# An encoder block whose instructions keep the program's order from the second gate on, with output blocks taken in pairs

## The chip, the cores and the metric

One core of one Trainium2 chip runs the whole kernel in one launch. The metric is the device time of that launch in microseconds. The kernel before took 1429.65 us, the median of three runs (1428.54 to 1430.14).

## The reference

One encoder block for 256 tokens of width 2048, in float32, cut to its products:

```python
h = rms_norm(x, g_mix); proj = h @ w_in              # q, k, v of three mixers, and 3 gates x 2048
oa = dilated windows (6 heads); ob = grouped attention (6 heads, 2 of k and v)
mkv = rms_norm(mem, g_mem) @ w_mem_kv                # 2048 -> 512 keys + 512 values
oc = cross-attention to mem (4 heads)
merged = gate0 * (oa @ w_br_a) + gate1 * (ob @ w_br_b) + gate2 * (oc @ w_br_c)   # gates: sigmoid
x = x + merged @ w_o                                 # 2048 x 2048
hf = rms_norm(x, g_ffn) @ w_ffn_in                   # 2048 -> 2 x 5632
x = x + (silu(hf[..., :5632]) * hf[..., 5632:]) @ w_ffn_out
```

## The kernel before

**Precision.** Every float32 operand goes as two float32r parts: `whi`, a rounded copy made by ACT (`split`, L86), and `wlo`, the remainder by DVE (L87). A product is three matmuls: high by high, high by low, low by high. So each weight costs ACT one pass and DVE one, and PE three for each half of the tokens (128 of 256). `xT`, `memT`, `mT`, `x1T`, `hT` are the stationary operands, transposed and split the same way; `rawT` is an operand as it is loaded.

**A plain product** (`product`, L161) makes 512 output columns: it loads four 128-row blocks of weights at a time (`raw`, 1 MB on SP's queue, three buffers), splits them two at a time into `whi` and `wlo` of 128x1024 (four buffers each), and gives PE 12 matmuls of 128x512 for each pair, into two PSUM banks, one per half of the tokens. The memory products (2 blocks), the projection to q, k, v (8), the gates (12), the branches (12), `w_o` (4) and the second feed-forward product (3 parts of 4) are all such.

**A feed-forward block** (`in_seven`, L525; 11 of them) makes 512 columns of the gated half and 512 of the other together, from eight K-steps of 256 rows. Steps written `d` go plainly, 24 matmuls into the banks Y, V (first column half) and Z, Q (second). Steps 0 to 2 are written `s`: the 2x2 of (K half, token half, column half) is done with seven products in place of eight. For these DVE combines weight blocks (`t2`, `t3`, `t4`, and one in place in `raw`), which are split like any weight, and the stationary side is combined once, in `stationary_forms` (L507: `fh`, `fl`). The entries 6, 7 and 4 of the list are products of the combined weights, over all three steps; X and W are banks of shared products. `ORDER` is the list for a block, `ORDER0` that of the first:

```python
ORDER = "s0 d3 s1 d4 s2 d5 6 d6 7 d7 4".split()
ORDER0 = "d3 d4 d5 s0 s1 d6 s2 6 d7 7 4".split()
```

At the end of a block ACT and DVE add the shared products to the banks, into `SA` and `SB` (L609 to L614). Then come Silu on ACT, the product of the two halves by DVE with the row scale `r_f` (L624), PE's transposes of it into a bank `tp`, and their split into `hT`.

**Order.** The program is handed to a scheduler that may reorder each engine's instructions by its own estimate of times. Side work (heads, attention, row sums) is written as generators that `tick` moves on beside the products. PSUM has 4 banks for products (`mm`) and 4 for the rest (`at`); for the feed-forward 7 and 1. All weights come on SP's queue, `memT` and `xT` on ACT's.

## Time and profile before

| | |
|---|---|
| median of the runs | 1429.65 us |
| the profiled execution's own time, and its span | 1432.02 us, 1430.2 us |
| matmul (PE) busy | 1400.4 us, 98% |
| weight load (PEld) busy | 1151.6 us, 81% |
| VectorE (DVE) busy | 963.3 us, 67% |
| ScalarE (ACT) busy | 741.0 us, 52% |
| GpSimd (POOL) busy | 78.8 us, 6% |
| moved by DMA | 276.99 MB, 194 GB/s over the span |
| 1 MB of weights, issue to landing | 4.9 to 5.0 us |

The page gives busy time by engine and by line; "idle before" is the time an engine stood ahead of such an instruction, and what ended it. The waits view lists what ended an engine's idle time, the timeline single instructions with start and duration, and the windows view the busy time, instructions and granted clock of a stretch. The matmul on `memT` first starts at 6.0 us, on `mT` (the output projection) at 612.2, on `x1T` (feed-forward, first product) at 711.2 and on `hT` (second product) at 885.2.

## The change

`InOrder` stands in for the engines: while `on` is set, each instruction keeps its place in the program on its engine. It is set in `run`, which takes a stage's blocks as lists of steps and makes the operands of a step (loads, combinations, splits) three steps ahead of its matmuls. So run the memory products, and everything from the second gate on; the q, k, v projection and the first gate stay with the scheduler.

```diff
-PK, LOAD = 2, 4
+PK = 2
-ORDER = "s0 d3 s1 d4 s2 d5 6 d6 7 d7 4".split()
-ORDER0 = "d3 d4 d5 s0 s1 d6 s2 6 d7 7 4".split()
+ORDER = "d3 s0 d4 s1 d5 s2 6 d6 7 d7".split()
+ORDER0 = "d3 s0 s1 s2 6 7 d4 d5 d6 d7".split()
+AHEAD = 3
...
+                ins = op(*args, **kw)
+                if self.owner.on:
+                    self.owner.tc.keep_in_program_order(ins)
...
+    psum = ctx.enter_context(tc.tile_pool(name="psum", bufs=4, space=bass.MemoryType.PSUM))
...
+        raw = wp.tile([P, PK, NC], F32, name="raw", bufs=6)
+        c = k0 % PK * NC
+        nc.sync.dma_start(out=raw[:, :nk].rearrange("p k n -> p (k n)"), in_=src[k0 // PK][:, c:c + nk * NC])
...
-                nc.scalar.dma_start(out=raw, in_=src[k0 // 2].rearrange("p (k s) -> p k s", s=S))
+                nc.sync.dma_start(out=raws[k0], in_=src[k0 // 2].rearrange("p (k s) -> p k s", s=S))
...
+        def finish_seven():
+            SA, SB = tl["A"], tl["B"]
+            nc.vector.tensor_sub(SB[:, 0], ps["Z"], SB[:, 0])
+            nc.vector.tensor_add(SA[:, 1], ps["V"], SA[:, 1])
+            nc.vector.tensor_add(SA[:, 0], ps["Y"], SA[:, 0])
+            nc.vector.tensor_add(SB[:, 1], ps["Q"], SB[:, 1])
+            return SA, SB
...
+        def second(u):
+            def ready():
+                b1, b2 = held[u]
+                nc.vector.tensor_add(t3[:, u], b2[:, 0], b2[:, 1])
+                nc.vector.tensor_add(b2[:, 0], b2[:, 0], b1[:, 0])
+                nc.vector.tensor_add(t2[:, u], b2[:, 0], b2[:, 1])
+                hi, lo = halves(b2)
...
+        def third(u):
+            def ready():
+                b1 = held.pop(u)[0]
+                nc.vector.tensor_add(b1[:, 1], t2[:, u], b1[:, 1])
+                hi, lo = halves(b1[:, 1])
+                return lambda: mul("V", at(2 * u + 1, 1), hi[:, 0], lo[:, 0])
...
+        steps = []
+        for o in order:
+            u = int(o[1:] or 0)
+            steps += {"d": lambda: [whole(u, 0), whole(u, 1)], "s": lambda: [first(u), second(u), third(u)],
+                      "6": lambda: [rest("6", v) for v in range(0, seven, 2)],
+                      "7": lambda: [rest("7", v) for v in range(0, seven, 2)]}[o[0]]()
...
+    def run(pairs):
+        nc.on = True
+        waiting = []
+        for p in pairs:
+            for products in p:
+                waiting.append(products)
+                if len(waiting) > AHEAD:
+                    waiting.pop(0)()
+                    tick()
...
+    def beginning():
+        start(hold(5, row_sums(a["mem"], r_m, 3, "mem")))
+        start(hold(10, constants()))
+        start(hold(8, fetch(xT, 1)))
+        yield pair(block_pair(a["w_mem"], 0), memT, whole_k(KT // 2),
+                   lambda c, r: start(take_slots(r, MEM_SLOTS[4 * c:4 * c + 4], r_m, "mem", nc.vector)), operand=memT)
+    run(beginning())
...
+                def hidden(av, bv):
+                    tl = s8([P, 2, 4, S], "hT", pool=tail)
+                    hT.append(tl)
+                    for t in range(T):
+                        nc.scalar.activation(av[:, t], av[:, t], AF.Silu, scale=r_f[:, 0, t:t + 1])
+                    def later():
+                        yield 2
+                        nc.vector.tensor_mul(av, av, bv)
+                        yield 2
+                        yield from transposed([av[:, t] for t in range(T)],
+                                              lambda k, m: (tl[:, 0, k:k + m], tl[:, 1, k:k + m]), lag=2)
+                    start(later())
```

`pair` replaces `in_seven`, and also takes two plain blocks together: a step `d` is two steps of 12 matmuls (`whole`), one for each column block, and `s` is three (`first` and `second` with 6 matmuls, `third` with 3). Loads are 512 KB into six buffers, and all go on SP's queue. The combination `t4` is now made in place in `raw` by `third`, which has the place of entry 4. `finish_seven` empties the banks Z, V, Y, Q in one go at the block's last step; the row scale `r_f` moves from the product of the halves to the sum with `x` behind the second product. The product of the halves and the two groups of transposes follow two steps after one another. `stationary_forms` runs in the middle of `w_o`, and the banks stay 4 and 4, with X, Y, W on the side of `tp`. The host lays the two column halves of `w_ffn_in` one behind the other.

DVE between two feed-forward blocks, before. `SA`, `SB` belong to the old block, `raw` and `wlo` to the new; the numbered names are combined weights:

```order
L610 TENSOR_TENSOR SA<-SA,SB 128x512
L87 TENSOR_TENSOR wlo<-t_8044,whi 128x512
L611 TENSOR_TENSOR SA<-mmY,SA 128x512
L589 TENSOR_TENSOR t_8383<-t_8381,raw 128x512
L87 TENSOR_TENSOR wlo<-raw,whi 128x1024
L583 TENSOR_TENSOR t_8382<-raw 128x512
L613 TENSOR_TENSOR SB<-mmZ,SB 128x512
L614 TENSOR_TENSOR SA<-mmQ,SA 128x512
L584 TENSOR_TENSOR raw<-raw 128x512
L624 SCALAR_TENSOR_TENSOR SA<-SB,scales,SA 128x512
L87 TENSOR_TENSOR wlo<-raw,whi 128x1024
L612 TENSOR_TENSOR SB<-mmV,SB 128x512
```

And after, where each instruction stands on the wrapper's line L70:

```order
L70 TENSOR_TENSOR SB<-mmZ,SB 128x512
L70 TENSOR_TENSOR SA<-mmV,SA 128x512
L70 TENSOR_TENSOR SA<-mmY,SA 128x512
L70 TENSOR_TENSOR SB<-mmQ,SB 128x512
L70 TENSOR_TENSOR t_8303<-raw 128x512
L70 TENSOR_TENSOR raw<-raw 128x512
L70 TENSOR_TENSOR t_8302<-raw 128x512
L70 TENSOR_TENSOR wlo<-raw,whi 128x1024
L70 TENSOR_TENSOR SA<-SA,SB 128x1024
L70 TENSOR_TENSOR raw<-t_8302,raw 128x512
L70 TENSOR_TENSOR wlo<-raw,whi 128x512
L70 TENSOR_TENSOR wlo<-raw,whi 128x1024
L70 TENSOR_TENSOR hT<-tp,hT 128x512
```

Before, the additions that empty the banks stand between the splits of the new block. After, all four stand in one piece, ahead of the three additions and the split of the new block's step `s0`, and the product of the halves (`SA<-SA,SB`) right behind that split; the split of the first transposed half (`hT<-tp,hT`) stands behind two more `wlo`.

PE at the same place, after, with the semaphores that an instruction waits on (those of DVE and ACT). First the turn from the first to the second step of `s0`:

```order
L70 MATMUL mmY<-whi,x1T 128x512
L70 MATMUL mmY<-wlo,x1T 128x512
L70 MATMUL mmY<-whi,x1T 128x512
L70 MATMUL tp<-ident,SA 128x128 [waits DVE_49,Activation_49]
L70 MATMUL tp<-ident,SA 128x128 [waits Activation_49]
L70 MATMUL tp<-ident,SA 128x128 x2
L70 MATMUL mmW<-whi,fh 128x512 [waits Activation_49]
```

And from its third step to the next step, of `d4`:

```order
L70 MATMUL mmV<-whi,x1T 128x512 [waits Activation_49]
L70 MATMUL mmV<-wlo,x1T 128x512 [waits DVE_49]
L70 MATMUL mmV<-whi,x1T 128x512
L70 MATMUL tp<-ident,SA 128x128 [waits DVE_49]
L70 MATMUL tp<-ident,SA 128x128 x3
L70 MATMUL mmY<-whi,x1T 128x512 [waits Activation_49]
```

The old block's first transposes (of `SA`) stand between the first and the second step of the new block's `s0`, the second group behind its third step, and `d4` behind that. Before, the scheduler placed them.

ACT at the end of the memory products, before; `sq`, `y` and `V` read the products' banks and free them:

```order
L309 ACTIVATE sq<-mm 128x512
L201 DMA rawT<-in_xT 128x512
L309 ACTIVATE sq<-mm 128x512
L86 ACTIVATE whi<-raw 128x1024
L201 DMA rawT<-in_xT 128x512
L86 ACTIVATE whi<-raw 128x1024
L89 ACTIVATE xT<-rawT,gT 128x256 x4
L86 ACTIVATE whi<-raw 128x1024
L201 DMA rawT<-in_xT 128x512 x2
L86 ACTIVATE whi<-raw 128x1024 x2
L89 ACTIVATE xT<-rawT,gT 128x256 x4
L324 ACTIVATE y<-mm,hf 128x128 x8
```

And after, where `mmY`, `mmV` are the banks of the first memory block and `mmZ`, `mmQ` those of the second:

```order
L70 ACTIVATE sq<-mmY 128x512
L70 ACTIVATE sq<-mmV 128x512
L70 ACTIVATE rows,rss<-rows 128x1024
L70 ACTIVATE xT<-rawT,gT 128x256 x2
L70 ACTIVATE whi<-raw 128x1024 x4
L70 ACTIVATE rows,rss<-rows 128x1024
L70 ACTIVATE V<-mmZ,scales 128x128
L70 ACTIVATE V<-mmQ,scales 128x128
L70 ACTIVATE rows,rss<-rows 128x1024
L70 ACTIVATE V<-mmZ,scales 128x128
```

The four `whi` in one piece are the token product's first; between the squares (`sq`) and the copies that free the banks (`V`, then `y`) now stand the row sums of `mem` and of `x` (`rows`), some of `xT` and those four.

## What the change will do to the time

> **What bounds the kernel now.** I read the page first, then PE's own waits, then PE's timeline for the pitch of its matmuls.

> ```profile
> span 1430.2 us, 16503 instructions
> PE 1400.4 (98%) x6323; PEld 1151.6 (81%) x6323; DVE 963.3 (67%) x1191; ACT 741.0 (52%) x971; POOL 78.8 (6%) x146
> ...
> PE mm L183 <- ACT memT L89: 13.4, 3, 7.0
> PE mmY L548 <- DVE rs_h L96: 5.6, 1, 5.6
> ```

> PE is the bound, and hardly waits: 13.4 us on the memory operand at the start, 5.6 us once between output projection and feed-forward, small change beside. But busy time hides something, so the pitch is needed (start, duration):

> ```profile
> 400.18 0.39 PE L184 MATMUL mm<-wlo,xT 128*128 128x512 f32 x1
> 400.41 0.39 PE L185 MATMUL mm<-whi,xT 128*128 128x512 f32 x1
> ...
> 712.17 0.63 PE L550 MATMUL mmY<-whi,x1T 128*128 128x512 f32 x1
> 712.59 0.63 PE L548 MATMUL mmV<-whi,x1T 128*128 128x512 f32 x1
> ...
> 1068.76 0.27 PE L229 MATMUL tp<-ident,SB 128*128 128x128 f32 x1
> 1068.87 0.27 PE L229 MATMUL tp<-ident,SA 128*128 128x128 f32 x1
> ```

> A 128x512 matmul starts 0.227 us after the one before (0.39 is its latency), a transpose 0.11. Behind the 5.6 us wait the pitch is 0.43: the clock. Stage by stage (PE, PEld, DVE, ACT, POOL busy; granted clock; DMA share; GB/s):

> ```profile
> 10.00:15.00 5.00, 3.09 (x14) 2.12 (x12) 1.25 (x3) 1.71 (x4) 0.00 (x0) 1.00 1.03 415
> 15.00:20.00 5.00, 0.00 (x0) 0.00 (x0) 1.99 (x8) 5.00 (x10) 0.00 (x0) 0.57 0.79 300
> 20.00:25.00 5.00, 4.64 (x10) 3.28 (x11) 3.87 (x15) 2.15 (x5) 0.00 (x0) 0.50 0.65 194
> 25.00:30.00 5.00, 5.00 (x21) 3.84 (x21) 4.58 (x7) 3.67 (x6) 0.00 (x0) 0.91 0.80 263
> 65.00:70.00 5.00, 3.90 (x21) 3.00 (x21) 4.44 (x3) 1.43 (x2) 1.08 (x1) 1.00 1.00 226
> 75.00:80.00 5.00, 3.87 (x18) 2.86 (x17) 3.40 (x13) 5.00 (x14) 0.00 (x0) 1.00 0.71 284
> 705.00:711.00 6.00, 0.57 (x6) 0.33 (x4) 6.00 (x13) 2.73 (x8) 0.00 (x0) 0.80 0.53 175
> 711.00:716.00 5.00, 4.82 (x13) 3.89 (x14) 4.66 (x15) 1.48 (x1) 0.00 (x0) 0.56 0.00 0
> 750.00:760.00 10.00, 9.09 (x40) 7.00 (x39) 9.88 (x13) 7.85 (x10) 0.00 (x0) 1.00 0.13 32
> 800.00:810.00 10.00, 9.22 (x39) 6.78 (x38) 10.00 (x12) 4.70 (x6) 0.00 (x0) 1.00 0.61 210
> 1019.70:1062.50 42.80, 42.74 (x192) 35.02 (x192) 37.88 (x46) 25.71 (x31) 0.00 (x0) 1.00 0.56 196
> ```

> So there are two places to win: the first 80 us (a 7 us hole at 12.7, 10 matmuls in 20 to 25 instead of 22, holes at 65 and 75) and 700 to 810 (holes of 5.4, 0.9 and 0.8 us, 13 matmuls instead of 22 in 711 to 716). The last row is one feed-forward block: 183 matmuls and 8 transposes, 183 x 0.227 + 8 x 0.11 = 42.4 us, in 42.8. Nothing is left there, but DVE is busy for 37.9 of it. That row decides this change.

> **What the change moves.** PE's work stays: 5,856 wide matmuls, 464 small ones in both. What changes is who stands behind whom. From the second gate on each engine keeps program order, with operands made three steps ahead of PE (four buffers of `whi` and `wlo`). Durations, and start-to-start times where an engine runs on:

> ```profile
> L87 DVE TENSOR_TENSOR wlo<-raw,whi 128x1024 fp32r<-128x1024 f32 x495 | 611.2, 1240 | 389.4 <-ACT whi L86 388.1
> L613 DVE TENSOR_TENSOR SB<-mmZ,SB 128x512 f32<-128x512 f32 x11 | 7.6, 687 | 0.0
> L516 DVE TENSOR_TENSOR ffull<-x1T 128x1024 f32<-128x1024 f32 x1 | 1.2, 1219 | 0.0
> L86 ACT ACTIVATE whi<-raw 128x1024 fp32r<-128x1024 f32 x495 | 522.8, 1062 | 571.9 <-PE mm L185 367.1 <-PE mmQ L550 81.8 <-PE mmV L550 60.0
> L86 ACT ACTIVATE whi<-t 128x512 fp32r<-128x512 f32 x33 | 20.7, 628 | 1.6 <-PE mmQ L550 1.6
> L623 ACT ACTIVATE SB<-SB,scales 128x512 f32<-128x512 f32 x11 | 8.0, 726 | 3.5 <-DVE SB L612 3.2
> ...
> 1062.95 2.36 DVE L87 TENSOR_TENSOR wlo<-raw,whi 128x1024 fp32r<-128x1024 f32 x2
> 1096.58 0.69 DVE L611 TENSOR_TENSOR SA<-mmY,SA 128x512 f32<-128x512 f32 x1
> 1097.18 0.68 DVE L589 TENSOR_TENSOR t<-t,raw 128x512 f32<-128x512 f32 x1
> ...
> 1070.74 0.68 DVE L584 TENSOR_TENSOR raw<-raw 128x512 f32<-128x512 f32 x1
> 1071.54 1.06 ACT L86 ACTIVATE whi<-raw 128x1024 fp32r<-128x1024 f32 x1 [0.92 <-DVE raw L584]
> ...
> 1076.18 1.06 ACT L86 ACTIVATE whi<-raw 128x1024 fp32r<-128x1024 f32 x1 [1.67 <-PE mmQ L550]
> 1077.27 1.23 DVE L87 TENSOR_TENSOR wlo<-raw,whi 128x1024 fp32r<-128x1024 f32 x1 [0.64 <-ACT whi L86]
> ```

> On DVE, 128x1024 takes 1.24 us and gives way after 1.13; 128x512 takes 0.69 and gives way after 0.60. DVE to ACT costs 0.12 us (1071.42 to 1071.54), ACT to DVE 0.03.

> *(a) One feed-forward block behind another: eight times.* Let PE start the new block's step 0 at T = 0. Steps 0 and 1 are d3 (12 matmuls, 2.72 us each), 2 and 3 the first and second of s0 (1.36 each), 4 its third (0.68), 5 and 6 d4, and so on. DVE has `wlo` for steps 0 to 2 and must now first do the four additions that empty the old banks, since they stand ahead of step 3: from 0.2 to 2.6. Then step 3: three additions to 4.4; its `whi` may begin 0.12 after the second of them (3.9), and lasts to 5.1; DVE stands idle for 0.7 and makes `wlo` to 6.2. Next in its queue is the product of the old block's halves (128x1024, Silu's 2 x 0.72 on ACT long done): to 7.45. PE finished step 2 at 6.8 and has the old block's first transposes next: **0.7 us lost**. Step 4: addition to 8.05, `whi` 0.63 to 8.8, `wlo` to 9.5, another hole of 0.87 on DVE. Step 5: `whi` behind that to 9.8, `wlo` to 11.0; then the split of the transposed half, to 11.7. PE ended step 4 at 10.05, and its next instruction is the second group of transposes, which needs the bank that this split empties: of four banks Y, X and W are in use. **1.6 us lost.** From here DVE has no lead. A d and an s cost PE 8.84 us; DVE 3 x 1.13 (d and the first), 1.8 + 1.13 + 0.7 (second), 0.6 + 0.6 + 0.87 (third) and 0.4 to the next `whi`: 9.5. So step 10 waits 0.5, step 15 0.65, step 17 0.6; from then on PE has more work than DVE, and the block ends with the lead restored. Sum 4.1 us: 46.5 against 42.8 before, **+3.7, eight times +30**. Bounds: were DVE's holes (0.7, 0.87, 0.4) filled by other work as they are before, DVE alone would reach the second transposes at about 9.7 against PE's 9.3, so 0.4 a block and no loss; half as much again on every wait gives 6.2, +46. I take the walk, since each of its hand-overs is a row.

> *(b) Blocks 4 and 8*, behind an output product, have no old halves: steps 10, 15 and 17 alone wait, 1.5 us against some 0.5: **+2** (0 to +3).

> *(c) From the output projection into the first block.* What stalled PE for 5.6 us is gone from there: the forms are made in the middle of the projection. But the new order has s0 s1 s2 6 7 in one piece. DVE must do in a row: 2 additions (1.2), eight splits of x1T, the row scale (16 small ones), three seconds and thirds with their holes (3 x 5.7), two firsts (2.3), four `wlo` of 6 and 7 (3.5), and 0.4 three times:

> ```profile
> 707.91 0.86 DVE L90 SCALAR_TENSOR_TENSOR x1T<-tp,gT,x1T 128x256 fp32r<-128x256 f32 x2
> ...
> 711.68 0.16 DVE L102 SCALAR_TENSOR_TENSOR rs_t<-rs_y 128x2 f32<-128x2 f32 x1
> 711.88 0.16 DVE L103 TENSOR_TENSOR rs_t<-rs_t,rs_v 128x2 f32<-128x2 f32 x1
> ```

> that is 8 x 0.4 and 16 x 0.2: 31.7 us together. PE has 21.5 (d3, three s, 6, 7 and four groups of transposes), and the last of DVE's pieces leaves it 1.1 more to do: some 11.5 us lost, 0.8 more where 7 must wait until X is copied behind 6, and a hole over 5 us (behind the row scale) that costs the clock as it did at 711, 2.0. That is 14.3 against before's 5.4 of hole, 2.0 of slow clock (9 starts missing of 22) and 2.1 in the two later windows (4 and 5 missing of 44): 9.5, so **+5** (-9, if everything is hidden, to +9).

> *(d) Merge and projection as pairs*: DVE has 1.13 of work per 2.72 of PE, and lead enough for the forms (7.3 us in one piece against 8.2 of lead). Before loses some 2 us there to transposes: **-1** (-2 to +2).

> *(e) The start.* One operand load now serves two blocks, 1.3 MB for 5.44 us of PE instead of 0.75 MB for 2.72, so the hole at 12.7 and its slow clock (7.0 + 2.7) should go. The first weights come as 512 KB rather than 256 KB and their `wlo` is 1.24 instead of 0.69: about 1.2 later. Against this stands the hand-over to the token product. Both memory blocks now end together, three of the four product banks are taken, and ACT has four `whi` and a row of squares, waiting for its transfer, ahead of the copies that free them. PE can do one half (24 matmuls, 5.4 us) of four steps; the scales come some 8 us, the copies 14 us after the memory products. About 8 lost, and the clock 2, against 2.2 to 4 now (windows at 65 and 75): **-3** (-11 to +6).

> Sum 30 + 2 + 5 - 1 - 3 = +33. The profiled execution took 1432.0 us, 1.8 over its span and 2.4 over the median of the runs; 33 more than it would be 1465, and as its excess is not the kernel's I add the 33 to the median 1429.65: 1463.

> The row of 750 to 760 shows that PE can stand for 0.9 us and keep clock 1.00; 705 to 716 that 5.6 us cost it. The waits of (a) lie between. [...]

> **The rivals.**
> 1. *DVE keeps up, and the kernel gets faster.* In the row of the block it has 4.9 us to spare, the new order has two additions less per block, and if ACT's `whi` come while DVE has other work the holes vanish. It decides below 0.9 us of waits per block. Then (a) and (b) cost nothing, (c) -9, (d) -2, (e) -3: 1416. Against it: in the new order `wlo` stands directly behind the addition its `whi` waits for, with nothing between. Chance 0.2.
> 2. *Half of it.* Waits of 2 us a block (+13), (c) -7, (e) -6: no change, 1430. Chance 0.05.
> 3. *The start is bound by transfers.* Weights go in halves:

> ```profile
> raw<-in_w_ffn SPq DMA_DIRECT2D x88, 1024.0 KB, 4.9
> ...
> raw<-in_w_mem SPq DMA_DIRECT2D x15, 512.0 KB, 4.7
> ```

> half the bytes take nearly the time there, and SP waits for a free operand buffer with all weights queued behind. 14.7 MB (the weights' 8.4, by their shapes, and 2.1 each of memT, mem and xT) are wanted in the memory products' 43.5 us (192 matmuls); at the 263 GB/s of 25 to 30 that is 56, (e) becomes +10: 1476. [...] Chance 0.05.
> 4. *The clock oscillates in the feed-forward.* Five waits a block of up to 1.6 us, the first two close together, trip it: eight times the 2.7 us that 12 missing starts cost in 20 to 25, +22: 1485. [...] Chance 0.05.

> **How the numbers follow.** The forecast has 0.65 and a range of its own from 1446 to 1480. About 0.2%, 2.9 us, can be told from no change here. Faster is rival 1, 0.2; same is rival 2, 0.05; slower is the rest, 0.75. The range must reach into rival 1's upper part: 1422 to 1480 leaves out some three quarters of 1, and 4.

> **What would show it.** In the profile after: feed-forward blocks of 46 to 47 us; PE's waits led by `tp` and `mmY`/`mmX` on DVE `wlo`, `hT` and `SA`; two holes of 1 to 2 us close behind each block's start; a hole of some 5 us in the first block; none at 12 to 20 us but one near 58; clock 1.00 elsewhere. Blocks under 43.7 us would prove the walk wrong.

## The result, and the profile after

The changed kernel took 1479.71 us, the median of four runs (1476.21 to 1480.60), against 1429.89 for the kernel before in the same runs: a ratio of 1.0339, 95% interval 1.0312 to 1.0366. It is slower by some 50 us. The prediction had 1463, slower with a chance of 0.75, and a range whose end of 1480 the result just meets. The profiled execution took 1478.82 us.

The page's first lines, and the first rows of PE's waits (total us, times, longest):

```profile
span 1477.0 us, 17243 instructions
PE 1422.2 (96%) x6323; PEld 1152.0 (78%) x6323; DVE 969.8 (66%) x1190; ACT 732.4 (50%) x981; POOL 76.6 (5%) x146
...
PE tp L70 <- DVE hT L70: 10.8, 8, 1.4
PE mmY L70 <- ACT whi L70: 6.4, 1, 6.4
PE mmY L70 <- DVE wlo L70: 5.5, 10, 1.8
PE mmW L70 <- ACT whi L70: 3.8, 1, 3.8
PE mm L70 <- ACT xT L70: 3.4, 1, 3.4
PE mmX L70 <- DVE wlo L70: 3.3, 11, 0.5
PE mmW L70 <- DVE x1T L70: 2.8, 1, 2.8
PE tp L70 <- DVE SA L70: 2.6, 8, 0.3
```

As many matmuls as before, DVE and ACT about as busy, and yet 47 us more: PE waits. Idle time shows only 25 of the 47 (54.8 us in place of 29.8); the other 22 are in PE's busy time, since a matmul's row lasts 0.39 us where the next, with nothing to wait for, starts after 0.227, and 0.63 where the granted clock is 0.50. The waits on the transposes (`tp`) come eight times each, once for each turn from one feed-forward block to the next. The 6.4 us in the second row are the start of the program and no loss.

By the first matmul on each operand (`memT`, `xT`, the second gate, `mT`, `x1T`, `hT`) the trace is cut into stages. Where the scheduler lets two stages overlap (some 2.5 us in the feed-forward of the last two rows), the cut is where the earlier one ends. Lengths in us of the two kernels and of four of the runs below:

```
                      memory token  merge  w_o   4 blocks out   4 blocks out   3 blocks out
before                56.6   318.3  231.3  99.0  174.0    88.8  169.6    88.8  126.6    71.2
after                 51.5   321.3  232.5  92.2  199.4    88.8  182.7    88.8  136.0    77.4
combinations earlier  51.1   321.3  232.5  92.2  195.1    88.8  176.2    88.8  131.3    79.3
order by hand         50.8   322.9  232.5  92.2  189.2    88.8  170.0    88.8  127.2    72.3
feed-forward unpinned 52.1   321.3  232.5  92.2  177.2    88.3  172.3    88.3  129.2    70.6
mixed                 51.0   321.3  232.5  92.2  175.7    88.8  169.2    88.8  126.9    70.8
```

The feed-forward blocks cost 25.4 + 13.1 + 9.4 = 47.9 us more, the last output stage 6.2; the memory products and the output projection win 5.1 and 6.8, the token product and the merge lose 3.0 and 1.2. One block, in the same columns as the prediction's windows, and the worst stretch of the first block:

```profile
1044.80:1091.26 46.46, 43.97 (x192) 34.62 (x191) 38.40 (x45) 25.14 (x32) 0.00 (x0) 1.00 0.57 181
717.00:730.00 13.00, 9.32 (x29) 6.47 (x28) 9.94 (x27) 3.95 (x6) 0.00 (x0) 0.76 0.30 81
730.00:742.00 12.00, 8.45 (x26) 6.21 (x27) 9.75 (x13) 8.21 (x12) 0.00 (x0) 0.72 0.26 88
```

46.46 us for what took 42.80, at a granted clock of 1.00: no clock is lost in an ordinary block. In the first block PE starts 55 instructions in 25 us, where 110 would fit 0.227 us apart, and there the granted clock is 0.76 and 0.72.

The turn itself, DVE first (start, duration, and in brackets the idle time ahead and who ended it), then PE's first matmul of the new block and its two groups of transposes:

```profile
1037.30 0.68 DVE L70 TENSOR_TENSOR t<-raw 128x512 f32<-128x512 f32 x1
1038.02 0.69 DVE L70 TENSOR_TENSOR raw<-raw 128x512 f32<-128x512 f32 x1
1038.74 0.69 DVE L70 TENSOR_TENSOR t<-raw 128x512 f32<-128x512 f32 x1
1039.97 1.23 DVE L70 TENSOR_TENSOR wlo<-raw,whi 128x1024 fp32r<-128x1024 f32 x1 [0.54 <-ACT whi L70]
1041.12 1.22 DVE L70 TENSOR_TENSOR SA<-SA,SB 128x1024 f32<-128x1024 f32 x1
1042.25 0.69 DVE L70 TENSOR_TENSOR raw<-t,raw 128x512 f32<-128x512 f32 x1
1043.72 0.69 DVE L70 TENSOR_TENSOR wlo<-raw,whi 128x512 fp32r<-128x512 f32 x1 [0.78 <-ACT whi L70]
1044.67 1.23 DVE L70 TENSOR_TENSOR wlo<-raw,whi 128x1024 fp32r<-128x1024 f32 x1 [0.26 <-ACT whi L70]
1045.81 0.68 DVE L70 TENSOR_TENSOR hT<-tp,hT 128x512 fp32r<-128x512 f32 x1
...
1035.19 0.39 PE L70 MATMUL mmY<-whi,x1T 128*128 128x512 f32 x1
...
1042.48 0.63 PE L70 MATMUL tp<-ident,SA 128*128 128x128 f32 x4 [0.33 <-DVE SA L70]
1046.55 0.66 PE L70 MATMUL tp<-ident,SA 128*128 128x128 f32 x4 [1.35 <-DVE hT L70]
```

Three holes on DVE, and PE behind them. The first two are ended by ACT's copy of what DVE itself has just added, the third by the copy that stands behind the second of these on ACT.

The end of the program, on SP's queue:

```profile
1404.81 9.12 SPq L70 DMA_DIRECT2D raw<-in_w_ffn_out  x5
1431.20 1.00 SPq L70 DMA_DIRECT2D out<-x  x2
1432.30 0.41 SPq L70 DMA_DIRECT2D raw<-in_w_ffn_out  x1
1439.10 0.99 SPq L70 DMA_DIRECT2D out<-x  x2
1440.18 4.10 SPq L70 DMA_DIRECT2D raw<-in_w_ffn_out  x6
```

From about 1414 to 1432 SP issues no load: the next one stands behind a store that waits for DVE's sums.

## The experiments

**Theory A**: the feed-forward loses its time by the order that is written on DVE. What ACT must copy is added just ahead of the remainder that needs the copy, in one piece with the emptying of the banks, and DVE cannot make up what it loses there. **Rival B**: it is how much DVE has to do at a turn; **rival C**: the pinning as such, or the smaller loads.

In the expectations, "the first experiment" is the run with earlier combinations, "the fifth" the order by hand, and "the ninth run" that with one list for all blocks; "the run beside it" is the ninth too.

**Combinations one step earlier.** In `first`, behind its split, in place of `second` and `third`:

```diff
                 hi, lo = halves(b1)
+                nc.vector.tensor_add(t3[:, u], b2[:, 0], b2[:, 1])
+                nc.vector.tensor_add(b2[:, 0], b2[:, 0], b1[:, 0])
+                nc.vector.tensor_add(t2[:, u], b2[:, 0], b2[:, 1])
+                nc.vector.tensor_add(b1[:, 1], t2[:, u], b1[:, 1])
```

> The changed kernel, with the four combinations of a step s (the additions that make t3, the block in raw, t2 and the last one in raw) issued one step earlier, right behind the split of first; second and third only split. No work is added or removed; DVE gets no instruction that waits for an ACT copy of what DVE has just added. Theory A (the order on DVE and its holes between addition, ACT copy and remainder set PE's pace in the feed-forward): the waits of 0.7 and 1.5 us behind a block's start and those at later s steps go, a block takes about 43 us in place of 46.4, the first block loses some 6 us less: about 1440 us (1434 to 1450). Rival B (what counts is how much DVE has to do at the boundary between blocks, holes or not): a third of it, about 1468. Rival C (loads of 512 KB, or the clock): no change, 1480.

Measured: 1462.79 us (1462.03 to 1464.56), ratio 1.0235 (1.022 to 1.025): 17 us gained, between A and B and nearer to B. The stretch of four later blocks went from 182.7 to 176.2. The timeline at a turn, DVE and ACT, tells why not more:

```profile
1032.96 0.68 DVE L70 TENSOR_TENSOR SB<-mmQ,SB 128x512 f32<-128x512 f32 x1
1035.39 1.23 DVE L70 TENSOR_TENSOR wlo<-raw,whi 128x1024 fp32r<-128x1024 f32 x1 [1.75 <-ACT whi L70]
...
1033.08 1.34 ACT L70 ACTIVATE SA<-SA,scales 128x512 f32<-128x512 f32 x2 [5.87 <-DVE SA L70]
1034.32 2.51 ACT L70 ACTIVATE whi<-raw 128x1024 fp32r<-128x1024 f32 x3
```

The new block's `whi` could have been made early, but on ACT the old block's Silu stands ahead of it and waits for DVE's additions. The hole has moved from one hand-over to another, and grown.

**A longer lead** was to tell whether four steps in place of three, with five buffers of `whi` and `wlo` each, would cover the turn. It does not fit: the pool of the heads' operands asks for 32 KB per partition where 24.06 are left. What it would give stays open.

**Silu, product and transposes later, and nothing else.**

```diff
                     def later():
                         yield 2
+                        for t in range(T):
+                            nc.scalar.activation(av[:, t], av[:, t], AF.Silu, scale=r_f[:, 0, t:t + 1])
+                        yield 1
                         nc.vector.tensor_mul(av, av, bv)
                         yield 2
                         yield from transposed([av[:, t] for t in range(T)],
-                                              lambda k, m: (tl[:, 0, k:k + m], tl[:, 1, k:k + m]), lag=2)
+                                              lambda k, m: (tl[:, 0, k:k + m], tl[:, 1, k:k + m]), lag=4)
```

> The changed kernel with Silu, the product of the halves and the transposes later by one to three steps, as in the order by hand, and nothing else: the combinations stay where the change has them. By the terms of the prediction the two waits at the boundary (0.7 and 1.6 us) go and those at the s steps (0.5, 0.65, 0.6) stay: blocks of about 44.3 us in place of 46.4, 1462 (1457 to 1468). Rival (the lag on DVE comes back at the next step whatever is moved away): 1472 or more.

Measured: 1477.36 (1475.49 to 1478.17), ratio 1.0334 (1.032 to 1.0349). The rival was right here. One block in the windows of this kernel, then the product and PE's first group of transposes at its turn:

```profile
1041.60:1087.70 46.10, 44.09 (x191) 34.74 (x191) 38.25 (x45) 24.97 (x32) 0.00 (x0) 1.00 0.55 183
...
1040.43 1.22 DVE L70 TENSOR_TENSOR SA<-SA,SB 128x1024 f32<-128x1024 f32 x1
...
1041.80 0.63 PE L70 MATMUL tp<-ident,SA 128*128 128x128 f32 x4 [1.04 <-ACT whi L70]
```

Of 2.3 us of waits that were to go, 0.4 went. The second group of transposes waits no longer, but the first now waits 1.04 us in place of 0.33. It reads the product, which stands behind the remainder of step 4 here and ends at 1041.65, 0.15 ahead of the transposes; the view names ACT, but this is DVE's delay. Here PE's waits on a late DVE gave DVE time; taken away at one place, they came back at another.

**Both, and the combinations behind the emptying of the banks**, with the stores on GpSimd's queue:

```diff
+                behind.append(combine)                 # the four combinations
...
                 if len(waiting) > AHEAD:
                     waiting.pop(0)()
+                    while behind:
+                        behind.pop()()
...
-                                nc.sync.dma_start(out=out[t * P:(t + 1) * P, o], in_=x[t][:, o])
+                                nc.gpsimd.dma_start(out=out[t * P:(t + 1) * P, o], in_=x[t][:, o])
```

> The changed kernel, pinned as it is, with another order written down: the four combinations of a step s a step earlier but behind the additions that empty the old block's banks; Silu two steps later on ACT, out of the way of the new block's copies; the product of the halves and the transposes later by one to three steps; and the stores of the result on GpSimd's queue. Theory A (it is the order as written that costs, and DVE can keep up in another one): DVE has its remainder for step 3 at 6.2 us behind the block's start where PE wants it at 6.8, so a block takes about 42.8 us; with the stores 6 us and the first block's 6 us: 1435 (1428 to 1445). Rival B (only a scheduler that may reorder everything, PE's matmuls too, gets there): blocks of 44.5, about 1453.

Measured: 1441.68 (1439.7 to 1442.7), ratio 1.0083 (1.0068 to 1.0098). A block, in the windows:

```profile
1033.60:1076.45 42.85, 42.67 (x193) 35.06 (x192) 38.23 (x45) 25.43 (x33) 0.00 (x0) 1.00 0.60 197
```

42.85, as long as before, pinned, with the same 38.2 us of DVE's work and the same loads: A is shown for the ordinary blocks, and B and C are not what costs there. On four blocks the two edits gain 6.5 and 1.1 alone, and 12.7 together with the combinations set behind the emptying of the banks; no run has this third edit apart. The first block did not follow: its stretch still takes 189.2.

**The feed-forward in the scheduler's hands** (`nc.on = False` at the head of `feeding`).

> The changed kernel with the pinning switched off in the feed-forward alone: the scheduler may reorder there. In its order the second group of transposes of each old block moves behind the next step, and the rest stays nearly as written. Theory A (the order as written costs, pinned or not; DVE is behind by then, so that a wait removed comes back at the next step): 1470 to 1480, blocks of 45.5 us or more. Rival (pinning itself costs): blocks of 43 us, 1447.

Measured: 1430.39 (1428.44 to 1432.11), ratio 1.0004 (0.9994 to 1.0014): 49 us gained. The order that the expectation names was misread: the scheduler moves far more than the transposes. DVE at a turn:

```profile
1010.46 1.22 DVE L70 TENSOR_TENSOR wlo<-raw,whi 128x1024 fp32r<-128x1024 f32 x1
1011.60 0.68 DVE L70 TENSOR_TENSOR SA<-mmY,SA 128x512 f32<-128x512 f32 x1
1012.20 0.68 DVE L70 TENSOR_TENSOR SA<-mmV,SA 128x512 f32<-128x512 f32 x1
1012.80 1.21 DVE L70 TENSOR_TENSOR wlo<-raw,whi 128x1024 fp32r<-128x1024 f32 x1
1013.93 0.68 DVE L70 TENSOR_TENSOR SB<-mmZ,SB 128x512 f32<-128x512 f32 x1
1014.53 0.68 DVE L70 TENSOR_TENSOR SB<-mmQ,SB 128x512 f32<-128x512 f32 x1
1015.13 0.68 DVE L70 TENSOR_TENSOR raw<-t,raw 128x512 f32<-128x512 f32 x1
```

Additions and remainders alternate again, and no row here has a wait for ACT. It also mends the end (70.6 us) and most of the first block (177.2). With the run by hand this says: the pinning costs through the order it holds, and a good one can be held too.

**The stores on GpSimd's queue** (the last edit of the run by hand, alone).

> The changed kernel with the stores of the result issued from GpSimd's queue in place of SP's. Theory A: in the last 77 us no load starts from 1420 to 1431, since SP stands behind stores that wait for DVE's sums; without them the loads run on, and the last stage takes some 72 in place of 77.4 us: about 1474.5. Rival (PE waits there for the sums themselves, as both blocks of a pair end together): no change, 1480.

Measured: 1473.17 (1471.96 to 1473.62), ratio 1.0304 (1.0289 to 1.032); the last stage 72.3 in place of 77.4. As expected.

**Nothing pinned** (`nc.on = False` in `run`).

> The changed kernel with nothing pinned: pairs, 512 KB loads on one queue, early forms and the new orders, in the scheduler's hands. Theory A (what the change gains at the start and in the output projection comes from pairs, queue and early forms, not from pinning): 1425 to 1432, as with the feed-forward alone unpinned. Rival (pinning gains these 4 and 7 us): about 1441.

Measured: 1430.81 (1428.97 to 1434.69), ratio 1.001 (0.9999 to 1.0021), as with the feed-forward alone unpinned. The output projection keeps its gain without pinning (91.5). At the start theory A is wrong: the memory products and the token stage, which overlap here between 51 and 58 us, take 378.6 us together where the pinned ones take 372.8, so that pinning gains some 6 us there. The merge is 2.1 us shorter without it (230.4).

**Early forms in the kernel before** (`stationary_forms()` called behind the second block of `w_o`).

> The kernel before, with the combined stationary operands made behind the second block of the output projection in place of behind the fourth. Theory A (the stall of 5.6 us and the slow clock behind it come from DVE's forms at that place, and the change's 6.9 us there come from moving them): 1423 (1421 to 1426). Rival (the row scale and the last transposes stall PE there all the same): 1428 to 1430.

Measured: 1427.94 (1427.21 to 1429.87), ratio 0.9991 (0.9982 to 1.0000). The rival came nearer: PE's wait ahead of the first block went from 5.6 only to 4.3 us:

```profile
PE mmY L550 <- DVE x1T L90: 4.3, 1, 4.3
```

In both kernels this first matmul starts 0.15 us behind the end of the last split of `x1T` (711.18 and 711.03 in the kernel before, 708.22 and 708.07 here), so that the 5.6 us, which the view puts down to the row scale (`rs_h`), were a wait for that split too. Yet the step is `d3`, whose own part of `x1T` was split long before. `banks.close()` ends the PSUM pools of 4 and 4 banks there and opens those of 7 and 1, and in the program this matmul waits for the last reader of the old banks, which is that split. The changed kernel keeps its 4 and 4. No run keeps them in the kernel before, so what that alone is worth stays open.

**One list for all blocks**: on the kernel by hand, `ORDER0 = ORDER`, and `yield 3` for `yield 2` ahead of the transposes.

> The pinned kernel with the order by hand (the fifth experiment), and the first feed-forward block by the same list as the others (d3 s0 d4 s1 d5 s2 6 d6 7 d7) in place of d3 s0 s1 s2 6 7 d4 d5 d6 d7; the first transposes of an old block one step later. Theory A (the first block stalls since the row of three s steps gives DVE more to do than PE in one piece, while it still has the last splits of x1T): the first four blocks take 174 in place of 189 us, 1427 in all (1421 to 1432), within 0.2% of the kernel before or faster. Rival (what is left of the output projection on DVE stalls PE in any list): 1436 or more.

Measured: 1429.14 (1427.74 to 1431.14), ratio 1.0000 (0.9991 to 1.0009). The stretch of the first four blocks takes 179.2, ten less, not fifteen. What the later transposes gave of it is not told apart.

**The token operand earlier** (on that kernel, `hold(4, fetch(xT, 1))` for `hold(8, fetch(xT, 1))`).

> The kernel of the run beside it (order by hand, one list for all blocks), with the loads of the token operand xT begun four steps earlier, among the memory products. Theory A (the hole of 3.6 us near 63, and the slow clock behind it, are the wait for xT, whose splits stand on ACT behind row sums that wait for their transfer; the transfers have room in 30 to 50): the token stage is 3 to 5 us shorter, the memory products at most 1 longer: 1423 where the run beside it has 1427. Rival (the transfers bound the start as a whole): what the token stage wins the memory products lose, no change between the two.

Measured: 1441.19 (1439.43 to 1442.42), ratio 1.0083 (1.007 to 1.0095): 12 us slower than the run beside it, which neither theory foresaw. The windows of the run beside it, and then of this one (GB/s last):

```profile
36.00:46.00 10.00, 10.00 (x46) 8.29 (x45) 3.34 (x5) 3.85 (x6) 0.00 (x0) 1.00 0.52 197
46.00:56.00 10.00, 6.72 (x27) 4.63 (x26) 5.01 (x14) 6.61 (x13) 0.00 (x0) 1.00 0.91 339
...
36.00:46.00 10.00, 6.79 (x25) 4.67 (x24) 4.75 (x8) 5.42 (x9) 0.00 (x0) 0.89 0.64 212
46.00:56.00 10.00, 7.77 (x27) 5.68 (x26) 3.37 (x5) 3.95 (x6) 0.00 (x0) 0.84 0.73 234
```

The memory products got 11.5 us longer (61.5 for 50.0), the token stage 2.3 too (323.0 for 320.7). The transfers were not at their limit (212 GB/s against 339). SP's waits over the first 60 us of the run beside it, and the first 70 of this one, tell more:

```profile
SPq L70 <- DVE xT L70: 2.6, 1, 2.6
SPq L70 <- DMA rawT<-in_xT: 1.7, 3, 1.2
...
SPq L70 <- DMA rawT<-in_xT: 10.8, 6, 4.5
SPq L70 <- DVE xT L70: 7.0, 5, 2.5
```

The pieces of `xT` share two `rawT` buffers with `memT`; SP stands until one has landed and been split, some 13 us longer than before, and the weights behind it on the one queue come late. No run gives the operand more buffers, so that this is read from the waits alone.

**Two plain steps first in the first block** (the list d3 d4 s0 d5 s1 s2 6 d6 7 d7, and transposes behind `w_o` a step earlier).

> The pinned kernel by hand with one list for all blocks (the ninth run), with d3 d4 s0 d5 s1 s2 6 d6 7 d7 for the first block and the transposes behind the output projection one step earlier each. Theory A (what is left of the stall in the first block is banks X and W waiting for the last splits of x1T on DVE; two plain steps first give DVE time for these): the first four blocks take 174 in place of 179.2 us, 1424 (1420 to 1428), faster than both kernels. Rival (the transposes now wait for the square sums and x, and d4 for x1T): 1429 or more.

Measured: 1429.38 (1427.25 to 1433.63), ratio 1.0000 (0.9991 to 1.0009); first stretch 179.8. The rival was right: the stall moved and did not shrink. What is left of it, some 5 us over the kernel before on these four blocks, stays open.

**The scheduler with earlier combinations** (feed-forward unpinned, the first experiment's edit, the old first list).

> The changed kernel with the feed-forward unpinned, the four combinations of a step s a step earlier as in the first experiment, and the first block's list as before (d3 d4 d5 s0 s1 d6 s2 6 d7 7). Theory A: the first block loses 1 us in place of 4.7, the eight waits of 0.7 us at the boundary go: 1422 (1418 to 1428), faster than both kernels. Rival (the scheduler has nothing to gain from either): 1430.

Measured: 1428.28 (1425.67 to 1431.03), ratio 0.9994 (0.9985 to 1.0004): not told from the kernel before. The first stretch took 175.5, 1.7 less than with the feed-forward alone unpinned where more than 3.7 were hoped for, the last three blocks 130.0, 0.8 more.

**Mixed**: the kernel by hand with one list, but the first four blocks (old list) and the last output stage unpinned.

```diff
             hT = []
+            nc.on = c0 > 0
...
             last = c1 == KF // 4
+            nc.on = not last
```

> The same pinned kernel by hand (the ninth run), but the first four feed-forward blocks and the last four output blocks left to the scheduler, the first block by the old list, and the stores of the result on SP's queue again: each stretch in the way that was fastest in a run before. Sum of those stages: 1426.4 of span less 3.7 (175.5 for 179.2 in the first four blocks), less 1.7 (70.6 for 72.3 at the end): 1421 of span, 1423 (1420 to 1428). Rival (the scheduler, pinned around, orders the stretches otherwise): 1429 or more.

Measured: 1423.05 (1421.24 to 1425.19), ratio 0.9954 (0.9942 to 0.9967): faster than both kernels, by 6 us and 57. The two stretches come out as forecast, within 0.2 us each (last row of the table).

## Why the prediction was right, and where it was short

- *The order on DVE at a turn* (a): right in place and in size. It had 46.5 us a block and eight times 3.7; the windows have 46.46, and 3.66. Counted from the block's first matmul at 1035.19, its `wlo` of step 3, product, `wlo` of step 4 and second transposes were to start at 5.1, 6.2, 8.8 and 11.7; they started at 4.8, 5.9, 8.5 and 11.4. Each is 0.3 early, since DVE begins to empty the banks 0.3 us ahead of that matmul and not 0.2 behind it. From start to start the two groups of transposes lost 0.5 and 1.5 us where 0.7 and 1.6 stood. But the waits were written as terms with a cause each, as if each could be taken away alone. The run with later transposes speaks against that: they behave as one delay of DVE, and most of what was taken away came back. That such waits cost no clock no run had shown: the rows of before have 0.9 us at a granted clock of 1.00, 5.6 us at 0.80 and 0.56, and none between. In the windows of a block, with waits of up to 1.35 us, it is 1.00.
- *Blocks behind an output product* (b): a size. 13.1 - 3 x 3.66 = 2.1 on one, 9.4 - 2 x 3.66 = 2.1 on the other: +4.2 where +2 stood.
- *Into the first block* (c): the mechanism was right, the size short. The projection won 6.8, the first block lost 25.4 - 11.0 = 14.4: +7.6 where +5 stood. The list of what DVE must do has no holes at the splits of `x1T`; the trace has four of 0.54 us there. The hole behind the row scale measured 3.84 us where some 5 stood, but the clock fell to 0.50 twice, behind it and at 716. The thought that early forms clear PE's stall was wrong: alone in the kernel before they take 1.3 of its 5.6 us. In the changed kernel, whose PSUM banks stay as they are, `d3` runs on without a wait, and the stall moves behind it.
- *Merge and projection* (d): +1.2 where -1 stood, for the most part one wait at the first pair.
- *The start* (e): -1.7 where -3 stood. A hole came near 63, but for `xT`, not for the banks that the prediction named: on ACT its splits stand behind the squares of `x`, which wait for their transfer.
- *The end*: the step that was missing. The prediction had no term for the last output stage, where the result's stores now stand on one queue in program order ahead of the weights: +6.2, of which 5.1 came back with the stores elsewhere.

Sum: 29.3 + 4.2 + 7.6 + 1.2 - 1.7 + 6.2 = 46.8, the difference of the two spans. That the time came out inside the range was luck in part: two of the four runs took 1480.60, and the 6.2 us at the end, which no term stood for, are a third of what the forecast missed. The rival that DVE keeps up was refused by the order as written; the run by hand shows that in an ordinary block it was a matter of that order alone. The two additions less per block, on which that rival leaned, are not there: the windows of a block have 45 instructions on DVE for 46, since the product is made in one piece.

## What to carry to other kernels

Where program order is held, walk the engine that is nearly full through the turn between two blocks, with every hand-over to another engine and back: a remainder right behind the addition that its copy needs cost a hole each time here (0.54 and 0.78 us on DVE at a turn), and an engine with 38 us of work in a block of 43 has little room for these. Put other work between such a pair, on both engines; and do not expect to take the waits on the other side away one by one, since they can be one delay (of 2.3 us, 0.4 went). A queue in program order holds stores too (5.1 us here): what waits for a result must not stand ahead of loads.

## What the runs showed of the hardware

```profile
50.79:54.20 3.41, 1.51 (x6) 0.72 (x5) 1.90 (x3) 2.99 (x6) 0.00 (x0) 1.00 0.98 339
54.20:57.62 3.42, 3.42 (x10) 2.52 (x8) 2.56 (x9) 3.42 (x7) 0.00 (x0) 0.50 1.03 419
...
47.42:50.84 3.42, 2.31 (x10) 1.49 (x8) 0.37 (x1) 1.45 (x3) 0.00 (x0) 1.00 0.98 358
50.84:54.25 3.41, 2.65 (x12) 1.99 (x11) 2.62 (x4) 3.41 (x9) 0.00 (x0) 1.00 1.00 391
54.25:57.66 3.41, 1.14 (x4) 0.48 (x3) 3.31 (x12) 3.41 (x6) 0.00 (x0) 1.00 1.03 417
57.66:61.08 3.42, 3.42 (x9) 2.63 (x8) 3.39 (x7) 1.95 (x3) 0.00 (x0) 0.50 1.02 407
```

In the changed kernel two starts at 52.3 and 53.6 came 1.3 and 1.0 us late, both in the piece that ends at 54.20, in which PE was busy for 1.51 us, and the clock then fell to 0.50. In the run with one list PE stood about as long there, but 1.1 us of it ahead of 50.84 and 0.8 behind, and the clock stayed at 1.00. In the piece after that PE was busy for 1.14 us, and the clock fell behind it.

In the traces of the two kernels, from the first matmul on, the clock fell to 0.50 eight times, each time behind a piece at 1.00 with two to five matmul starts, and behind none with six or more, where 15 starts 0.227 us apart would fit. One wait of 1.76 us in the changed kernel, which ends at 381.38, left six starts in its piece and the clock at 1.00. The waits of 0.33 and 1.35 us at each turn left eight or more, and cost no clock.
